# Layer 1 of a two-layer decoder trunk on one core: one order list from keys to turn, scalings shared by three engines, adaLN gate summed through DRAM

## The chip, the cores and the metric

The kernel runs on one core of a Trainium2 chip. The metric is device time in microseconds (us) of one execution. TensorE (PE) has a row of its own for weight loads (PEld); the others are VectorE (DVE), ScalarE (ACT), GpSimd (POOL), and SyncE (SP), which here only issues DMAs. Every engine takes its instructions in order.

## The reference

The trunk has 256 tokens of width 1024 and two layers. Both do x = x + gate * mixer(rmsnorm(x) * (1 + scale) + shift), where shift, scale and gate come from c @ ada_w + ada_b. Layer 1 is sparse attention with 16 heads in 4 groups; layer 2 is a chunkwise mLSTM with 8 heads. A final RMSNorm follows. What matters here, cut from the reference:

```python
shift, scale, gate = jnp.split(c @ ada_w[i] + ada_b[i], 3, axis=-1)
h = rmsnorm(x, norm_g[i]) * (1.0 + scale[:, None, :]) + shift[:, None, :]
q, kv, gate_logits, z = jnp.split(h @ w_in, A_SPLITS, axis=-1)
k_cmp = compress_tokens(kv[:, :, 0], ...); v_cmp = compress_tokens(kv[:, :, 1], ...)
p_cmp = masked_probs(s_cmp, dist_c >= 0)        # compressed branch
p = masked_probs(s, mask)                       # selected branch, then the window branch
o = gates[:, :, 0] * o_cmp + gates[:, :, 1] * o_slc + gates[:, :, 2] * o_win
y = o.reshape(B, S, A_WIDTH) * jax.nn.silu(z)
x = x + gate[:, None, :] * (y @ w_out)
```

masked_probs is a softmax: exponentials of the scores less a row's extreme, divided by their sum. The products keep more than one float32r pass's precision: each factor is split into hi (rounded to fp32r) and lo (the rest), and a product is the three matmuls hi*hi, lo*hi, hi*lo.

## The kernel before, in words

Layer 1 is written with a manual schedule: an engine runs its instructions in the order in which the program text makes them. It has four stages. `first_phase` loads x and c and makes the modulated, transposed activations (to about 52 us). The key stage in `nsa` (to 71 us) multiplies them with eight blocks of key and value weights (`kv_block`, L539 to L541; the loop runs over all eight, and behind each it makes embeddings or splits queries). `attention` (to about 157 us) runs over eight pairs of heads n = 0 to 7, driven by the string ORDER: each word of it is one step, and the number behind it names the pair, the head j in it, and the branch. `turn` (to about 186 us) ends layer 1: output projection, residual, RMSNorm, transposition and the first products of layer 2. Layer 2 is ordered by a scheduler and runs to 421 us.

The steps of `attention`, with the lines of the profile: S, scores (PE, L754 and L757); m, a row's extreme (DVE, L773); e, exponential with its sum (ACT, L780); f, factors gate/sum (DVE, L786 to L788); the **scalings** s, p, q, which multiply 128x128 and 128x256 probabilities by a factor for each row (L794; s on DVE, p on POOL, q one branch on each); T, transposes of the scaled probabilities (PE, L799) and t, their copy out of PSUM (ACT, L624); V, probabilities times values, in matmuls packed by columns (PE, L816); C, the compressed branch (PE, L821); y, times the SiLU of z (DVE, L825); Y, hi and lo of y (L624, L829); z, the gate path (PE, L1610 to L1612), whose weights are split in two halves of 512 columns each by `make_hi` on ACT (L164) and `make_lo` on DVE (L169); out and last, the output projection (PE, L869); `hi` and `lo` alone split the next weights in the stream; d, a column of the shift and scale sums for layer 2 (DVE, L852).

The **gate of layer 1**: `gr` multiplies c by four weight blocks in column-packed matmuls (PE, L226, two halves of 512 columns), which leaves four partial rows on four partitions; `gc` copies them to SBUF (ACT); `gs` sums them and spreads the sum to all 128 partitions by a matmul with a 0/1 matrix `sel` in fp32 (PE, L859); `ga` adds it to the bias that an ACT-queue DMA has spread into `gate0` (DVE, L863; step `bias`, L855). `gate0` is first read by the residual's multiplication (DVE, L1067).

`turn` is ordinary code: for each half a of the tokens the residual (L1067, L1068), squares (ACT, L1111), the root (ACT L209, DVE L210 to L214), the normalisation (ACT L1115, DVE L1116), eight transposes (PE, L1125), the modulation (ACT L1137, DVE L1135), rounding to hi (DVE L1145, ACT L1143), the rest lo (DVE, L1149), and layer 2's first products (PE, L1158).

Weights come by DMAs on SP's queue, 512 KB each, in the order of a list `queue`, into a ring of buffers; POOL's queue carries small loads and layer 2's exchanges through DRAM scratch.

## Time and profile before

| what | value |
| --- | --- |
| time, median of 3 runs | 423.61 us (423.51 to 425.01) |
| profiled execution, its own time | 423.31 us |
| its span in the trace | 421.5 us |
| granted TensorE clock | 0.996 |
| PE, PEld busy | 98%, 85% |
| DVE, ACT, POOL busy | 83%, 64%, 23% |

The span is what the trace covers; 1.8 us of the execution's time lie outside it. A busy share is over the whole span. The chain of waits follows the work that ended last back to what released it. The groups of instructions give the count, the busy time and the mean duration of a form. The windows give busy times stage by stage. The DMA issues give the median time from issue to landing. On PE durations overlap, since matmuls are pipelined; the distance from one start to the next says what an instruction costs there.

### The profile page before, as it was taken

The numbers are of one execution on the slowest core, as the hardware profiler recorded it, in microseconds if no ns is written. First come the engines' busy times: TensorE is split into PE (matmuls) and PEld (weight loads), VectorE is DVE, ScalarE is ACT, GpSimd is POOL, SyncE is SP. The second block draws the span as 40 slices with busy tenths as digits, with TensorE's granted clock in tenths as the row PEclk, the third lists the DMA queues.
The fourth block names the chain that finished last, engine by engine and source line by source line (L and its number), as shares of the span: only waits on it lengthen the run. The fifth ranks groups of instructions, "written<-read, shape, count | busy, mean of one in ns | idle before, by whom it ended". The sixth has DMA issues, their size and how long they took to land.

```text
span 421.5 us, 7600 instructions
## 1 busy us (share of the span) xinstructions
PE 412.3 (98%) x2669; PEld 357.2 (85%) x2669; DVE 348.6 (83%) x736; ACT 270.8 (64%) x541; POOL 96.6 (23%) x154
## 2 busy tenths in 40 slices
PE   8999999999999999999999999999999999999994
PEld 5899999789778877878999999888888888888884
DVE  6999898999999998878592699899858998558554
ACT  6666693788987973668547966565456554565523
POOL 4000112354676750142223200000000240320000
PEclk9999999999999999999999999999999999999998
DMA  8999996963799678239667467467456587640002
GB/s 321 410 407 406 396 322 197 342 274 136 253 334 388 236 251 298 96 119 317 218 226 277 157 193 225 177 205 265 169 176 202 186 296 230 180 143 0 0 2 100
DMA packets 27543, 96.21 MB, mean 228 GB/s; under 512 B 3512, under 2 KB 3616, under 8 KB 27376
## 3 DMA queue, kind: packets, MB, share of 16 engines
q1 hardware_dynamic: 26208, 92.30, 61.9%
q0 software_dynamic: 1008, 2.63, 1.7%
q10 hardware_dynamic: 288, 0.79, 0.5%
q8 instruction: 21, 0.34, 0.3%
q14 instruction: 18, 0.15, 0.1%
HBM read 94.61 MB, written 1.09 MB: 227 GB/s over the span
## 4 chain that ended last, share of the span: by engine, by line
PE 84%; issue 5%; DMA 4%; POOL 2%; DVE 2%; ACT 1%; SPq 0%; DVEq 0%; POOLq 0%
PE bank L539 10%; PE bank L541 10%; PE bank L540 10%; PE bank L433 7%; PE bank L1612 6%; PE bank L1610 6%; PE bank L1611 6%; PE bank L1523 5%; PE bank L1036 5%; PE bank L1158 3%; DMA Q<-in_columns 3%; PE bank L799 2%; PE bank L1403 2%; PE bank L816 2%; PE bank L754 2%
## 5 line engine op out<-in xcount | busy, mean ns | idle before, releaser
L169 DVE TENSOR_TENSOR wl<-raw,wh 128x1024 fp32r<-128x1024 f32 (+4 forms) x127 | 139.3, 1112 | 34.5 <-ACT wh L164 33.8
L164 ACT ACTIVATE wh<-raw 128x1024 fp32r<-128x1024 f32 (+4 forms) x127 | 119.2, 957 | 65.1 <-PE bank L541 28.2
L539 PE MATMUL bank<-wh,one 128*128 128x512 f32 (+1 forms) x208 | 76.9, 370 | 0.0
L540 PE MATMUL bank<-wl,one 128*128 128x512 f32 (+1 forms) x208 | 76.3, 367 | 0.0
L541 PE MATMUL bank<-wh,one 128*128 128x512 f32 (+1 forms) x208 | 76.2, 367 | 0.0
L1610 PE MATMUL bank<-one,wh 128*128 128x256 f32 x208 | 59.6, 287 | 0.0
L1612 PE MATMUL bank<-one,wl 128*128 128x256 f32 x208 | 59.0, 284 | 0.1
L1611 PE MATMUL bank<-one,wh 128*128 128x256 f32 x208 | 58.8, 283 | 0.0
L794 POOL TENSOR_SCALAR Pr<-Pr,f 128x128 f32<-128x128 f32 (+1 forms) x42 | 46.7, 1128 | 32.9 <-DVE f L788 18.8
L539 PEld LDWEIGHTS bank<-wh,one 128*128 128x128 f32 x208 | 39.2, 188 | 6.2 <-DVE tz L511 0.2
L541 PEld LDWEIGHTS bank<-wh,one 128*128 128x128 f32 x208 | 39.2, 188 | 6.2
L540 PEld LDWEIGHTS bank<-wl,one 128*128 128x128 f32 x208 | 39.2, 189 | 6.0
L1610 PEld LDWEIGHTS bank<-one,wh 128*128 128x128 f32 x208 | 39.7, 191 | 1.4 <-issue 0.8
L1612 PEld LDWEIGHTS bank<-one,wl 128*128 128x128 f32 x208 | 39.7, 191 | 0.5 <-DVE wl L169 0.3
L1611 PEld LDWEIGHTS bank<-one,wh 128*128 128x128 f32 x208 | 39.8, 191 | 0.1
L780 ACT ACTIVATE Pr<-Pr,mn 128x128 f32<-128x128 f32 (+1 forms) x64 | 28.2, 444 | 4.3 <-DVE mn L773 4.3
L433 PE MATMUL bank<-one,wh 128*128 128x256 f32 x224 | 29.8, 284 | 0.5 <-ACT one L407 0.4
L433 PEld LDWEIGHTS bank<-one,wh 128*128 128x128 f32 x224 | 28.1, 192 | 0.9 <-ACT one L407 0.6
L160 POOL TENSOR_TENSOR raw<-raw,gate 128x256 f32<-128x256 f32 x16 | 13.6, 858 | 49.7 <-DMA raw<-in_out_b 24.9
L1384 DVE SCALAR_TENSOR_TENSOR conv<-bank,one,conv 128x255 f32<-128x255 f32 (+2 forms) x48 | 20.0, 466 | 2.1 <-ACT conv L1379 2.1
L852 DVE CUSTOM_DVE_ANT_0 raw<-raw,one,one 128x1024 f32<-128x1024 f32 x16 | 21.1, 1330 | 0.0
L773 DVE CUSTOM_DVE_ANT_0 Pr<-bank,one 128x128 f32<-128x128 f32 (+1 forms) x64 | 18.7, 348 | 0.0
(336 smaller groups left out, 793.1 us busy)
## 6 DMA issues: line engine op xcount, KB each, us to landing
raw<-in_wide SPq DMA_DIRECT2D x44, 512.0 KB, 4.4
raw<-in_units SPq DMA_DIRECT2D x18, 512.0 KB, 4.6
raw<-in_turn SPq DMA_DIRECT2D x16, 512.0 KB, 6.8
raw<-in_gates SPq DMA_DIRECT2D x16, 512.0 KB, 4.9
raw<-in_out_b SPq DMA_DIRECT2D x16, 512.0 KB, 3.9
raw<-in_start SPq DMA_DIRECT2D x8, 512.0 KB, 9.7
Q<-in_columns SPq DMA_DIRECT2D x8, 512.0 KB, 9.6
raw<-in_hidden SPq DMA_DIRECT2D x8, 512.0 KB, 4.3
```

What stands on the lines that cost most here:

```text
L164: self.nc.scalar.activation(v(hi), src, AF.Copy)
L169: self.nc.vector.tensor_sub(v(lo), src, v(hi).bitcast(F32))
L433: nc.tensor.matmul(out, w[:, ch * P : ch * P + P], h[:, kk], start=(kk == 0 and m == 0 and ch % 2 == 0), stop=(kk == 7 and m == 2), skip_g ...
L539: nc.tensor.matmul(out, self.hh[:, kk, sl], wh, start=first, stop=False, skip_group_check=True)
L540: nc.tensor.matmul(out, self.hh[:, kk, sl], wl, start=False, stop=False, skip_group_check=True)
L541: nc.tensor.matmul(out, self.hl[:, kk, sl], wh, start=False, stop=last, skip_group_check=True)
L780: nc.scalar.activation(v, v, AF.Exp, bias=mn[:, a, br, j : j + 1], scale=-1.0, accum_out=sm[:, a, br, j : j + 1])
L794: es[br].tensor_scalar(v, v, F[n][:, a, br, j : j + 1], None, op0=OP.mult)
L852: nc.vector.tensor_tensor_reduce(raw, raw, self.cbc, scale, self.pca[:, 72 + 8 * b + kc : 73 + 8 * b + kc], OP.mult, OP.add, self.cols1[s] ...
L1610: nc.tensor.matmul(out, wh, self.hh[:, kk], start=first, stop=False, skip_group_check=skip)
L1611: nc.tensor.matmul(out, wh, self.hl[:, kk], start=False, stop=False, skip_group_check=skip)
L1612: nc.tensor.matmul(out, wl, self.hh[:, kk], start=False, stop=last, skip_group_check=skip)
```

## The change

One list for layer 1 from the first key block to the turn: `kv_block` is cut in three parts for each block (`k:block,part`), queries (`qa`, `qb`), embeddings (`E`), and the evacuations (`kd`, `G`, `vo`) become words of ORDER; so do the turn's steps (`l` last, `r` and `rp` residual on DVE or POOL, `sq` square, `sc` root, `x` normalise, `tr` transpose, `md` modulate, `ro` rounded, `re` rest, `n` and `v` products, `nh` and `nl` splits). The whole of ORDER is new. Six of the eight key blocks are now loaded as part of the stream's `hi` words. The scalings are named by the engines of the two branches (`spv`: POOL and DVE; `saa`: ACT twice): POOL goes from 42 to 32 instructions, DVE from 22 to 14, and ACT has 18 as a copy with a factor from a column. The gate's two `sel` matmuls, its two additions and the spread of the bias by an ACT-queue DMA go; instead five DMAs on POOL's queue do the sum through DRAM: `g1` twice (a store of four rows), `g2` (a load as 32 x 4 x 32), a DVE sum and addition of the bias on 32 partitions (`g3`), `g4` (a store of 32x32), `g5` (a load of the whole row into all 128 partitions of `gate0`, 512 KB). The weights of z are laid out so that hi and lo are one instruction each of 1024 columns in place of two of 512. Line numbers move by about 15 to 20 (L794 becomes L816, L799 L821, L816 L838, L1067 L1093, L1135 L1151).

```diff
@@ make_hi
-        if kind == "z":
-            r4 = raw.rearrange("p k j (i d) -> p k j i d", i=2)
-            views = [((lambda w, i=i: w.rearrange("p (k i j d) -> p k i j d", k=4, i=2, j=2)[:, :, i]), r4[:, :, :, i]) for i in range(2)]
-        elif kind == "q":
+        if kind == "q":
...
@@ nsa
-        def kv_block(kk):
-
-            wh, wl = self.take()
+        kw, banks = [], {}
+
+        def kv_block(kk, part):
+
+            while len(kw) <= kk:
+                kw.append(self.take())
...
     ORDER = """
-    d:0,0 hidden:0 hi hidden:1 S:0,0 lo S:0,1 hi hidden:2 hidden:3 z:0,0 m:0,0 m:0,1 e:0,0 lo S:1,0 e:0,1 f:0 gelu:0 s:0,0 hi S:1,1 gelu:1
...
+    k:0,1 hi hi lo lo hi lo qa:3 k:0,0 k:0,2 k:1,0 d:0,0 qa:2 k:1,1 k:1,2 E:1,0 hi k:2,1 k:3,1 qb:3 hi k:2,2 k:2,0 k:3,0 k:4,0 lo lo E:0,0 hi lo E:1,1
...
+    l:0,0,6 l:0,0,7 r:0,0 sq:0,0 l:0,1,6 l:0,1,7 r:0,1 sq:0,1 l:1,0,3 l:1,1,3 l:1,0,4 nl:2 sc:0 l:1,0,5 x:0,1 nh:1 l:1,0,6 l:1,0,7 nl:1 l:1,1,4 rp:1,0
...
@@ attention
         def scaled(n, j, *es):
             for br in range(2):
                 for a in range(2):
-                    v = probs(n, j, br, a)
-                    es[br].tensor_scalar(v, v, F[n][:, a, br, j : j + 1], None, op0=OP.mult)
+                    v, f = probs(n, j, br, a), F[n][:, a, br, j : j + 1]
+                    if es[br] is nc.scalar:
+                        copy(v, v, scale=f)
+                    else:
+                        es[br].tensor_scalar(v, v, f, None, op0=OP.mult)
...
-        def gate_bias():
-            nc.scalar.dma_start(self.gate0, t["ada_b"][0:1, 2048:3072].partition_broadcast(P))
-
-        def gate_sum(bank):
-            b = B["gs"] = self.bank(bank)
-            nc.tensor.matmul(b, self.sel, W["A"].pop(0), start=True, stop=True)
-
-        def gate_add(n):
-            g = self.gate0[:, 512 * n : 512 * n + 512]
-            nc.vector.tensor_tensor(g, g, B["gs"], op=OP.add)
+        def four(A):
+            return A.rearrange("(j r) k -> j r k", r=32)[:, 0]
+
+        def gate_store(n):
+            if not n:
+                W["quarters"] = self.pd.tile([4, D], F32, name=self.nm("quarters"), tag="quarters")
+            nc.gpsimd.dma_start(W["quarters"][:, 512 * n : 512 * n + 512], four(W["A"].pop(("gate", n))))
+
+        def gate_load():
+            W["gq"] = T([32, 4, 32])
+            nc.gpsimd.dma_start(W["gq"], W["quarters"].rearrange("j (b c) -> b j c", b=32))
+
+        def gate_sum():
+            W["gv"] = T([32, 32])
+            nc.vector.tensor_reduce(W["gv"], W["gq"].rearrange("b j c -> b c j"), axis=AX.X, op=OP.add)
+            nc.vector.tensor_tensor(W["gv"], W["gv"], self.gbias, op=OP.add)
...
+            nc.gpsimd.dma_start(self.gate0, W["whole"].rearrange("b c -> (b c)").unsqueeze(0).partition_broadcast(P))
...
-               "s": lambda n, j: scaled(n, j, nc.vector, nc.vector), "p": lambda n, j: scaled(n, j, nc.gpsimd, nc.gpsimd), "q": lambda n, j: scaled(n, j, nc.vector, nc.gpsimd),
+               **{"s" + b + c: lambda n, j, b=b, c=c: scaled(n, j, by[b], by[c]) for b in "vpa" for c in "vpa"},
...
@@ turn
-        def last(a, half, ks):
-            for k in ks:
-                self.out_mm(k, *held[k], a, *pieces[a][half])
+        def last(a, half, k):
...
-        transposed(0)
-        for half in range(2):
-            last(1, half, [6, 7])
-        modulate(0)
-        hi(4)
-        rounded(0)
...
+        return {}, {"l": last, "sq": square, "sc": root, "x": scale, "tr": transposed, "md": modulate, "ro": rounded, "re": rest, "n": narrow, "v": wide,
...
-    out["path"] = flat([z[:, k, :, gp, :, ih] for ih in range(2) for gp in range(2) for k in range(2)])
+    out["path"] = flat([z[:, k, :, gp, :, ih].reshape(P, 4, 2, 2, 64).transpose(0, 1, 3, 2, 4) for ih in range(2) for gp in range(2) for k in range(2)])
```

Layer 2's order and `first_phase` up to its last instructions on PE are as they were. Three places where the rows moved:

PE at the first of the two gate sums, before. L226 are the packed rows of the gate, L757 and L754 the scores, L799 transposes, L859 the matmul with `sel` (`one_18` is that matrix, `adaA` the copied rows).

```order
L226 MATMUL bank_1605<-raw_1204,one_33_141 32x512
L757 MATMUL bank_1614<-KH_755,Q_946 128x256
L757 MATMUL bank_1614<-KL_756,Q_946 128x256
L757 MATMUL bank_1614<-KH_755,Q_946 128x256
L757 MATMUL bank_1614<-KL_756,Q_946 128x256
L799 MATMUL bank_1623<-one_16_89,Pr_1339 128x128 x3
L859 MATMUL bank_1637<-adaA_1629,one_18_94 128x512
L799 MATMUL bank_1642<-one_16_89,Pr_1504 128x128 x3
L754 MATMUL bank_1615<-KH_755,Q_946 128x512
L754 MATMUL bank_1615<-KL_756,Q_946 128x512
L754 MATMUL bank_1616<-KH_755,Q_946 128x512
L754 MATMUL bank_1616<-KL_756,Q_946 128x512
```

The same place in the change, behind the second half of the rows (now L223); L821 are transposes, L843 the compressed branch, L1578 the gate path.

```order
L223 MATMUL bank_1635<-raw_1518,one_33_140 32x512
L223 MATMUL bank_1635<-raw_1360,one_33_140 32x512
L223 MATMUL bank_1635<-raw_1460,one_33_140 32x512
L223 MATMUL bank_1635<-raw_1462,one_33_140 32x512
L223 MATMUL bank_1635<-raw_1518,one_33_140 32x512
L821 MATMUL bank_1662<-one_14_87,Pr_1508 128x128 x3
L821 MATMUL bank_1702<-one_14_87,Pr_1508 128x128 x3
L843 MATMUL bank_1532<-PcT_1582,one_264_1329 128x256
L843 MATMUL bank_1532<-PcT_1582,one_266_1330 128x256
L843 MATMUL bank_1532<-PcT_1582,one_264_1329 128x256
L843 MATMUL bank_1532<-PcT_1582,one_266_1330 128x256
L1578 MATMUL bank_1725<-one_4_70,wh_1162 128x256
```

No matmul with `sel` stands behind the rows any more, here or elsewhere: PE has 2136 rows in place of 2138.

POOL in the second half of `attention`, before: scalings of pairs 4 (`Pr_1631`, `Pr_1632`), one behind the other.

```order
L794 TENSOR_SCALAR Pr_1631<-Pr_1631,f_1752 128x128
L794 TENSOR_SCALAR Pr_1631<-Pr_1631,f_1752 128x256
L794 TENSOR_SCALAR Pr_1631<-Pr_1631,f_1752 128x128
L794 TENSOR_SCALAR Pr_1631<-Pr_1631,f_1752 128x256
L794 TENSOR_SCALAR Pr_1632<-Pr_1632,f_1752 128x128
L794 TENSOR_SCALAR Pr_1632<-Pr_1632,f_1752 128x256
L794 TENSOR_SCALAR Pr_1632<-Pr_1632,f_1752 128x128
L794 TENSOR_SCALAR Pr_1632<-Pr_1632,f_1752 128x256
```

POOL there in the change, from the store of the second half of the rows (L884) to the spread of the gate (L900); `Pr_1791` and `Pr_1792` are pair 5, `Pr_1946` pair 6, `Pr_2055` pair 7.

```order
L884 DMA quarters_1660<-adaA_1797 4x512
L888 DMA one_370_1827<-quarters_1660 32x4x32
L816 TENSOR_SCALAR Pr_1791<-Pr_1791,f_1872 128x128
L816 TENSOR_SCALAR Pr_1791<-Pr_1791,f_1872 128x256
L816 TENSOR_SCALAR Pr_1792<-Pr_1792,f_1872 128x128
L816 TENSOR_SCALAR Pr_1792<-Pr_1792,f_1872 128x256
L816 TENSOR_SCALAR Pr_1946<-Pr_1946,f_1979 128x128
L816 TENSOR_SCALAR Pr_1946<-Pr_1946,f_1979 128x256
L897 DMA whole_2150<-one_411_2006 32x32
L816 TENSOR_SCALAR Pr_2055<-Pr_2055,f_2146 128x128
L816 TENSOR_SCALAR Pr_2055<-Pr_2055,f_2146 128x256
L900 DMA gate_813<-whole_2150 128x1024
```

The load L888 reads what the two stores wrote, so it waits for the landing of the second, and the scalings of pairs 5 to 7 stand behind it on POOL.

DVE at the first half of the tokens in the turn, before, from the end of the root: L1116 normalises, `wl_2373` is the lo part of a 1024-column weight, L1135 modulates what PE transposed, L1145 rounds.

```order
L214 SCALAR_TENSOR_TENSOR rq_y_2362<-rq_a_2363,rq_y_2362 128x1
L1116 TENSOR_SCALAR Pr_2295<-one_2_69,rq_y_2362 128x512
L169 TENSOR_TENSOR wl_2373<-raw_2201,wh_2372 128x1024
L1135 TENSOR_SCALAR tz_2383<-bank_2382,cols_382_1915 128x128 x2
L1135 TENSOR_SCALAR tz_2383<-bank_2382,cols_424_2127 128x128 x2
L1145 CAST one_4_70<-tz_2377 128x4x128
L1067 TENSOR_TENSOR y_488_2413<-bank_2086,gate_813 128x512
L1149 TENSOR_TENSOR one_6_71<-tz_2377,one_4_70 128x4x128
L1067 TENSOR_TENSOR y_489_2418<-bank_2087,gate_813 128x512
L1068 TENSOR_TENSOR one_2_69<-one_2_69,y_489_2418 128x512
L1110 TENSOR_SCALAR ss_2224<-ss_2224,one_12_85 128x1
L1149 TENSOR_TENSOR one_6_71<-tz_2383,one_4_70 128x4x128
```

The same in the change (L1134 normalises, L1151 modulates, L1160 rounds, L1164 is the rest).

```order
L1134 TENSOR_SCALAR Pr_2326<-one_2_69,rq_y_2340 128x512
L166 TENSOR_TENSOR wl_2353<-raw_2170,wh_2352 128x816
L1093 TENSOR_TENSOR y_488_2371<-bank_2092,gate_813 128x512
L1151 TENSOR_SCALAR tz_2386<-bank_2385,cols_363_1789 128x128 x2
L1151 TENSOR_SCALAR tz_2386<-bank_2385,cols_433_2121 128x128 x2
L1160 CAST one_4_70<-tz_2376 128x4x128
L1164 TENSOR_TENSOR one_6_71<-tz_2376,one_4_70 128x4x128
L1093 TENSOR_TENSOR y_496_2427<-bank_2093,gate_813 128x512
L1094 TENSOR_TENSOR one_2_69<-one_2_69,y_496_2427 128x512
L1164 TENSOR_TENSOR one_6_71<-tz_2386,one_4_70 128x4x128
L1125 TENSOR_SCALAR ss_815<-ss_815,one_12_85 128x1
```

The 1024-column lo ahead of the modulation is gone; an 816-column one and the multiplication of the residual (L1093) stand there.

More of the change, by code (lines that the diff above doesn't have):

```diff
@@ L1107, in square, with narrow_hi, narrow_lo @@
+        def narrow_hi(n):
+            half_made[n] = self.make_hi(self.first + n)
+        def narrow_lo(n):
+            self.make_lo(*half_made.pop(n))
+            self._load()
+        def last(a, half, k):
+            while len(held) < k - 1:
+                n = len(held) + 2
+                held[n] = self.take(hold=n > 2)
+            self.out_mm(k, *held[k], a, *self.pieces[a][half])
         def square(a, half):
[L1108 removed]
@@ L1223, in turn, with narrow @@
-        rest(1, 0)
-        rest(1, 1)
-        lo(5)
-        w.append((4, self.take(hold=True)))
-        products(vs[0], w[2:], 0, 512, (0, 1))
-        products(bs[1][:, 0:272], first, 1, 272)
-        GT = self.T(pc, [P, 2, 16])
-        for a in range(2):
-            nc.vector.tensor_tensor(GT[:, a], bs[a][:, 256:272], self.bif, op=OP.add)
+        def narrow(a, m):
+            if not first:
+                first.extend((3 * n, self.take(hold=n > 0)) for n in range(3))
+            if not m:
+                bs[a] = self.bank(6 + a)
+            products(bs[a][:, 0:272], first, a, 272, (m,))
@@ L1233, in todo, with wide, gates @@
+        def wide(m, n):
+            if not vs:
+                vs.update((a, self.bank(4 + a)) for a in range(2))
+            while len(w) <= n:
+                w.append((2 * len(w), self.take(hold=True)))
+            products(vs[0], w[n : n + 1], 0, 512, (m,))
+        def gates(a):
+            if "t" not in half_made:
+                half_made["t"] = self.T(pc, [P, 2, 16])
+            nc.vector.tensor_tensor(half_made["t"][:, a], bs[a][:, 256:272], self.bif, op=OP.add)
         def todo():
```

311 lines of the change are left out of this document (129 added, 182 removed).

## The prediction

> **What bounds the kernel now.** First the page's busy times, then the chain of waits, because busy times alone do not say who waits for whom.
>
> ```profile
> PE 412.3 (98%) x2669; PEld 357.2 (85%) x2669; DVE 348.6 (83%) x736; ACT 270.8 (64%) x541; POOL 96.6 (23%) x154
> PE 84%; issue 5%; DMA 4%; POOL 2%; DVE 2%; ACT 1%; SPq 0%; DVEq 0%; POOLq 0%
> ```
>
> PE is 98% busy and carries 84% of the chain. The windows show whether another engine is as full where the change works:
>
> ```profile
> 90.00:110.00 20.00, 20.00 (x189) 15.99 (x188) 19.45 (x70) 16.83 (x54) 12.96 (x14) 1.00 0.36 129
> 110.00:130.00 20.00, 20.00 (x158) 15.99 (x157) 19.79 (x63) 15.71 (x51) 13.72 (x14) 1.00 0.94 344
> 130.00:150.00 20.00, 19.79 (x143) 16.30 (x143) 19.83 (x62) 17.52 (x49) 12.78 (x11) 1.00 0.79 293
> ```
>
> (Length, then PE, PEld, DVE, ACT, POOL; then clock, DMA share, GB/s.) DVE is as full as PE from 90 to 150 us, so who waits for whom decides. PE's waits from 52 to 187 us:
>
> ```profile
> PE bank L1158 <- DVE one L1145: 0.5, 1, 0.5
> PE bank L816 <- DVE y L825: 0.2, 1, 0.2
> PE bank L1158 <- DVE one L1149: 0.2, 1, 0.2
> ```
>
> PE waited 0.9 us in 135. DVE is full but keeps ahead. So layer 1 is as long as PE's list of matmuls, and only two things shorten it: fewer or cheaper matmuls, or these waits. The Trainium skill, Perfetto Trace Analysis, Identifying the Most-Contended Engine, says that matmul busy time is a bad measure because matmuls are pipelined, and that weight-load busy is the better one. By it PE would have 15% in hand (85%), and DVE would count as bound here; the 0.9 us of waits do not agree.
>
> **The change part by part.**
>
> *Gate sums off PE.* The order of the rows takes two fp32 matmuls with `sel` from PE and adds none.
>
> ```profile
> 109.82 0.67 PE bank L757 x4
> 110.49 0.33 PE bank L799 x3
> 110.82 0.98 PE bank L859 x2
> ...
> 113.39 0.47 PE bank L757 x4
> ...
> 129.66 0.86 PE bank L859 x2
> ```
>
> They held the chain for 0.98 + 0.86 = 1.84 us. Nothing lay beside them that PE waits for, so all of it goes: **-1.84**.
>
> *Fewer packed runs.* Four L757 matmuls take 0.67 us behind the packed L226, and 0.47 behind transposes: 0.20 for each return from a packed run. In the new order packed runs stand next to one another (a gate half beside V, V:6 beside V:7): by the rows of PE's order 9 runs in place of 11. **-0.4** (bounds 0 and 0.8, if entering a run costs as much as leaving it).
>
> *Waits that PE has.* One is at V:6 (L816 above), the others in the turn. Its timeline there:
>
> ```profile
> 170.93 0.85 PE L869 MATMUL bank<-KL,Q 128*128 128x512 f32 x3
> 171.61 0.84 PE L869 MATMUL bank<-KH,Q 128*128 128x512 f32 x3
> 172.52 1.24 PE L1158 MATMUL bank<-wh,one 128*128 128x272 f32 x8
> ...
> 179.71 1.09 PE L1158 MATMUL bank<-wh,one 128*128 128x512 f32 x4
> 181.29 0.97 PE L1158 MATMUL bank<-wh,one 128*128 128x272 f32 x5 [0.49 <-DVE one L1145]
> ```
>
> Three L869 go from start to start in 0.68 (170.93 to 171.61), 0.23 each. The run from 171.61 should have given way at 172.29 and did at 172.52: a fourth wait of 0.2 that has no bracket. The four matmuls from 179.71 take 0.93, so the last wait is 181.29 - 180.64 = 0.65, bracket and restart. In the turn that is 0.2 + 0.2 + 0.65 = 1.05, and 0.2 at V:6.
>
> Now each in the new order. V:6 waits for y:2's reading of its bank; in the new list five groups of three transposes (at 0.33) and nine projections (at 0.23) stand between `y:2` and V:6, 3.7 us: the 0.2 goes. In the turn, before the transposes 21 projections (4.9 us) stand behind the residual's last input where 18 did (4.2), so the root has 0.7 more. Between the first transposes and the products stand 9 matmuls (2.1 us) where 12 did (2.8), but what DVE has to do there is less:
>
> ```profile
> 169.53 1.23 DVE L169 TENSOR_TENSOR wl<-raw,wh 128x1024 fp32r<-128x1024 f32 x1 [1.15 <-ACT wh L164]
> 170.68 1.36 DVE L1135 TENSOR_SCALAR tz<-bank,cols 128x128 f32<-128x128 f32 x4
> 171.96 0.41 DVE L1145 CAST one<-tz 128x512 fp32r<-128x512 f32 x1
> ...
> 174.20 1.07 DVE L1068 TENSOR_TENSOR one<-one,y 128x512 f32<-128x512 f32 x1
> ...
> 175.64 0.68 DVE L1149 TENSOR_TENSOR one<-tz,one 128x512 fp32r<-128x512 f32 x1
> ```
>
> The modulation stood behind a lo of 1.23 us that itself waited 1.15 for ACT. Without it modulation and rounding are 1.36 + 0.41 and some 0.3 of handing over, 2.1 us against 2.1 of cover: about 0.1 left. In the second half 8 matmuls of 512 columns (1.9 us) cover what 6 (1.4) did: 0.65 falls to about 0.2. The L1149 wait: behind the rounding DVE now has a rest, a residual (a multiplication like L863 below and L1068) and the second rest, 0.68 + 0.68 + 1.07 + 0.68 = 3.1, and PE has 20 products of 272 columns (0.13 each: eight from 172.52 to 173.60) and two of 512 ahead of the need, 3.1: about 0.1 left. Together 1.05 becomes 0.4; with V:6 that is **-0.85** (bounds: -1.25, and 0 if as much comes back).
>
> *Scalings.*
>
> ```profile
> L794 POOL TENSOR_SCALAR Pr<-Pr,f 128x256 f32<-128x256 f32 x21 | 28.4, 1353 | 0.0
> L780 ACT ACTIVATE Pr<-Pr,mn 128x256 f32<-128x256 f32 x32 | 15.8, 498 | 3.2 <-DVE mn L773 3.2
> L794 POOL TENSOR_SCALAR Pr<-Pr,f 128x128 f32<-128x128 f32 x21 | 19.0, 904 | 32.9 <-DVE f L788 18.8 <-ACT PT L624 11.0 <-PE bank L799 3.2
> L780 ACT ACTIVATE Pr<-Pr,mn 128x128 f32<-128x128 f32 x32 | 12.4, 390 | 1.1 <-DVE mn L773 1.1
> L794 DVE TENSOR_SCALAR Pr<-Pr,f 128x256 f32<-128x256 f32 x11 | 4.4, 400 | 0.0
> L794 DVE TENSOR_SCALAR Pr<-Pr,f 128x128 f32<-128x128 f32 x11 | 3.9, 356 | 0.1
> ```
>
> POOL gives up five pairs (5 x 2.26 = 11.3 us), DVE four (3.0 us), ACT takes nine. ACT has no such form in this trace. Below: DVE's pair, 356 + 400 = 0.76; above: POOL's, 2.26 (20 us in all). I take the exponentials, same engine and shapes, also with a column as operand: 390 + 498 = 0.89 a pair, 8.0 us in all. ACT was busy 16.8 + 15.7 + 17.5 = 50.1 of 60 us from 90 to 150, and not every second of the 8 falls there. z gives some back:
>
> ```profile
> L164 ACT ACTIVATE wh<-raw 128x512 fp32r<-128x512 f32 x16 | 9.1, 628 | 0.0
> L164 ACT ACTIVATE wh<-raw 128x1024 fp32r<-128x1024 f32 x6 | 6.2, 1057 | 0.0
> L169 DVE TENSOR_TENSOR wl<-raw,wh 128x512 fp32r<-128x512 f32 x16 | 10.7, 708 | 0.0
> L169 DVE TENSOR_TENSOR wl<-raw,wh 128x1024 fp32r<-128x1024 f32 x6 | 7.4, 1247 | 0.0
> L863 DVE TENSOR_TENSOR gate<-gate,bank 128x512 f32<-128x512 f32 x2 | 1.4, 676 | 0.0
> ```
>
> 16 x 628 - 8 x 1057 = 1.6 us off ACT; 16 x 708 - 8 x 1247 = 1.4 off DVE. DVE also loses L863's 1.4 and gains a sum over 32x4x32 and an addition, of which I have no row: between 0.36 (one scaling of 128 columns) and 1.4 (as both L863), I take 0.7, as one L863. DVE is lighter by 3.0 + 1.4 + 1.4 - 0.7 = 5.1 us, ACT heavier by 6.4, POOL lighter by 11.3. None of the three holds the chain, so all this is worth **0** in itself: PE's matmuls hide it. If that cover is gone on ACT, 50.1 + 6.4 = 56.5 of 60 us still fits, but the copies t then queue behind scalings. For places with little lead in the new order (pair 3's transposes right behind its DVE scaling, out:0 into banks that m:7,1 has to free) I add **+0.3** (bounds 0 and 3).
>
> *The gate through DRAM.* The prices of such hops:
>
> ```profile
> raw<-in_start SPq DMA_DIRECT2D x8, 512.0 KB, 9.7
> DT<-in_final_g POOLq DMA_DIRECT2D x1, 512.0 KB, 4.8
> drawer<-one POOLq DMA_DIRECT2D x1, 16.0 KB, 3.6
> ```
>
> What POOL spends on an issue, and what PE does meanwhile:
>
> ```profile
> L1343 POOL DMA_DIRECT2D QK<-drawer x4 | 2.2, 559 | 3.2 <-DMA drawer<-one 3.2
> ```
>
> ```profile
> 124.00 2.75 PE bank L816 x32
> ...
> 128.07 0.94 PE bank L754 x4
> ```
>
> g2 waits on POOL for the landing of g1's second store, 3.6 us by `drawer`, and the scalings of pairs 5 to 7 queue behind it; T:5,0,0 waits for the first of them (2.26). From the transposes that gate the copy of the rows to T:5,0,0 PE has two heads' scores (0.94 + 0.47 each), four words of z and C:1 (at 0.12 a 128x256 matmul 12 and 4 of them: 1.44 each, 0.48), 32 packed (2.75) and four L799 (1.3): some 13 us. The wait asks for t and the copy (no more than the 0.63 of a 512-column split each), 3.6, an issue of 0.56 and 2.26: 7.7. So 5 us are left. Then g4 (3.6) lies beside 5.8 us (twelve projections, five groups of transposes, 16 packed of V:5), and g5 (4.8) beside 7.7 (32 packed of V:6 and V:7, C:3, transposes, 18 projections) until L1067 wants the gate; behind g5 on POOL only one residual queues. **0**, with bounds of 0 and the lateness priced below. The Trainium skill speaks against the change here: DMA: Bandwidth & Descriptors, Anatomy of one DMA, says that a DMA's semaphore wait is done on the issuing sequencer before dispatch, and gives 2.0 us + bytes/436e3 a hop, most of it a receipt from memory. That would make 2.0 of the 3.6; the `drawer` row is dearer, and the row decides.
>
> *Key stage, layer 2.* The same key matmuls in another order; the waits of PE quoted at the start hold none from it: **0**. Layer 2's rows are the same.
>
> **Sum:** -1.84 - 0.4 - 0.85 + 0.3 = -2.8. The span goes from 421.5 to 418.7; with the 1.8 us outside it 420.5, against 423.3 for this profiled execution. The median of the runs stood 0.3 above it; runs scatter by about as much, so I add 0.1: **420.6**, against 423.4 on the same footing.
>
> **The rivals.** (1) *Only the matmuls go*: every wait removed comes back elsewhere, since the same chains between DVE, ACT and PE are only put in another order. For it: DVE is at 19.8 of 20. Against it: DVE is lighter by 5. 423.4 - 1.84 = 421.6. (2) *ACT becomes late*: a scaling ahead of a copy t on ACT delays the transposed probabilities; six of the nine pairs late by half a pair's scaling, 0.45, take back 2.7: 423.3. For it: 56.5 of 60 us. Against it: ACT's scalings take 0.9 where POOL's took 2.3. (3) *DVE was the bound after all*, as the skill's weight-load rule would have it: the time falls with DVE's 5.1 us, 423.4 - 5.1 = 418.3; the waits speak against it. (4) *Slower: the gate arrives late*. Place: g4 and g5 on POOL's queue and then L1067. From when: both with their issues longer than 5.8 + 7.7 and the root's 0.7, 14.2 us. By the rows they take 3.6 + 4.8 + 1.1 = 9.5. Were both as slow as 512 KB at the start (9.7, DMA engines full), they would take 20.5, be 6.3 late, and give 426.9. For it: DMA shares of 0.79 to 0.94 from 110 to 150. Against: the POOL queue's row of the same size has 4.8. (5) The change does not do what it says: excluded for PE, whose order shows the matmuls gone.
>
> **How the numbers follow.** Forecast 0.60 (419.3 to 421.6), rival 1 0.14, rival 2 0.11, rival 3 0.06, rival 4 0.09. About 0.5% (2.1 us) is what a measurement of this kernel tells from no change: faster is below 421.5, slower above 425.7. Faster: nearly all of the forecast (0.56), half of rival 1 (0.07), rival 3: 0.69. Same: the rest of both (0.11) and rival 2: 0.22. Slower: rival 4, 0.09. The range runs from rival 3 to just past rival 2, 418.3 to 423.7, and leaves out rival 4 and the ends of the others; the forecast alone is 419.3 to 421.6.
>
> **What would show it.** Right: no matmul of 128x512 between transposes behind the packed gate rows; PE's waits from 52 to 187 us at 0.5 or less in sum; the scaling on ACT near 390 and 498 ns; POOL idle some 3 us at g2 with PE not waiting for T:5,0,0; no DVE wait for `gate` before its first residual. Wrong: PE waits for PT (ACT's copies) or for `one` in the turn of 0.5 and more, or DVE idle at L1093 for a DMA. If the time is above 421.6, the step that failed is the +0.3 for tight places or the -0.85.

## The result, and the profile after

The changed kernel takes 421.38 us (median of 6 runs, 420.66 to 422.19), against 423.61 for the kernel before on the same chip (6 runs, 423.50 to 425.01): a ratio of 0.994, 95% interval 0.9922 to 0.9957. The forecast was 420.6 with a range of 418.3 to 423.7. The profiled execution took 421.66 us, its span is 419.9, and the granted clock is 0.996 as before.

The page of the changed kernel, busy times and shares of the chain of waits:

```profile
PE 409.9 (98%) x2665; PEld 355.9 (85%) x2665; DVE 344.7 (82%) x720; ACT 276.0 (66%) x551; POOL 92.3 (22%) x149
PE 90%; DMA 4%; ACT 2%; DVE 1%; issue 1%; SPq 1%; DVEq 0%; ACTq 0%
```

PE is 2.4 us less busy, and its share of the chain rose from 84% to 90%. The total lies in the forecast; where it comes from is not what was forecast. PE's timeline shows it at three places: the first matmul of the key stage, layer 2's first matmul behind the turn, and the last matmul of the kernel. Before:

```profile
52.38 0.28 PE L1610 MATMUL bank<-one,wh 128*128 128x256 f32 x1
...
192.27 0.39 PE L540 MATMUL bank<-wl,one 128*128 128x512 f32 x1
...
415.76 0.28 PE L1523 MATMUL bank<-late,V 128*128 128x256 f32 x1
```

After:

```profile
52.22 0.36 PE L540 MATMUL bank<-wh,one 128*128 128x256 f32 x1
...
188.71 0.39 PE L541 MATMUL bank<-wl,one 128*128 128x512 f32 x1
...
414.09 0.28 PE L1491 MATMUL bank<-late,V 128*128 128x256 f32 x1
```

From the key stage to the end of the turn (called layer 1 below) PE took 192.27 - 52.38 = 139.89 us, and now takes 136.49: **-3.4**, where -2.8 was forecast. From there to the last matmul it took 223.49 and now takes 225.38: **+1.9**, where nothing was forecast, since layer 2's rows are the same. So two questions stand: why layer 2 became slower, and of what the -3.4 is made.

**Layer 1.** PE's waits between 50 and 192 us, by the view of waits:

```profile
PE bank L1173 <- ACT wh L161: 0.5, 1, 0.5
PE bank L821 <- ACT PT L643: 0.3, 1, 0.3
```

The view leaves out short idle times; from start to start they show. Measured so, the four waits that were to be shortened cost 0.22 + 0.36 + 0.65 in the turn and 0.37 at V:6, 1.6 us. Three are gone, and the one of 0.65 (PE at 176.75, behind the rounding) is down to 0.19: 1.4 us went. Two others came. The first is at 118 us, where the transposes of pair 3 need a bank that ACT has to copy out first. The chain of waits there (start, length, what):

```profile
105.33 1.85 PE bank L223 x16
107.18 0.43 PE bank L821 x3
107.62 6.34 DMA raw<-in_path
...
113.98 1.06 ACT wh L161
115.04 1.97 ACT Pr L799 x8
117.01 0.95 ACT wh L161
117.96 0.38 ACT PT L643
...
118.47 0.52 PE bank L821 x3
```

Read from below: the transposes waited for the copy (L643), the copy stood on ACT behind a split of weights (L161), that behind exponentials and a first split, and the first split behind its weights, which landed at 113.96. SP's queue had waited for a buffer that the packed gate rows (L223) read until 107.2. One late load thus holds up a `hi` that the order puts ahead of a copy, and a copy that PE needs stands behind it. The second wait is in the turn:

```profile
177.17 4.49 PE bank L1173 x27
...
181.69 1.07 ACT wh L161
...
182.80 4.91 PE bank L1173 x20
```

The split at 181.69 writes a buffer that the narrow products (272 columns) read until then, and PE needs its result at once. From start to start these two waits cost 0.46 and 0.69; at the same place before stood 0.23.

### The profile page after: what moved, and what is told of

Read it like the earlier page. It is cut to its first block, busy times and chain, and to the rows that moved or that the text cites. A ratio compares the mean times of both kernels' runs of the same rounds, so it can differ in the third digit from the quotient of the medians.

```text
span 419.9 us, 7581 instructions
## 1 busy us (share of the span) xinstructions
PE 409.9 (98%) x2665; PEld 355.9 (85%) x2665; DVE 344.7 (82%) x720; ACT 276.0 (66%) x551; POOL 92.3 (22%) x149
## 4 chain that ended last, share of the span: by engine, by line
PE 90%; DMA 4%; ACT 2%; DVE 1%; issue 1%; SPq 1%; DVEq 0%; ACTq 0%
PE bank L540 10%; PE bank L542 10%; PE bank L541 10%; PE bank L430 8%; PE bank L1580 6%; PE bank L1578 6%; PE bank L1579 5%; PE bank L906 5%; PE bank L1491 5%; PE bank L1062 5%; PE bank L1173 4%; PE bank L838 3%; PE bank L821 2%; DMA Q<-in_columns 2%; PE bank L1371 2%; PE bank L575 2%
## 5 line engine op out<-in xcount | busy, mean ns | idle before, releaser
L161 ACT ACTIVATE wh<-raw 128x1024 fp32r<-128x1024 f32 (+3 forms) x119 | 118.4, 1008 | 72.2 <-PE bank L542 35.6
L540 PE MATMUL bank<-wh,one 128*128 128x512 f32 (+2 forms) x208 | 77.8, 374 | 0.0
L541 PE MATMUL bank<-wl,one 128*128 128x512 f32 (+2 forms) x208 | 77.0, 370 | 0.0
L542 PE MATMUL bank<-wh,one 128*128 128x512 f32 (+2 forms) x208 | 76.8, 370 | 0.0
L1578 PE MATMUL bank<-one,wh 128*128 128x256 f32 x208 | 59.3, 285 | 0.0
L816 POOL TENSOR_SCALAR Pr<-Pr,f 128x128 f32<-128x128 f32 (+1 forms) x32 | 37.6, 1195 | 32.4 <-DVE f L807 22.4
L1578 PEld LDWEIGHTS bank<-one,wh 128*128 128x128 f32 x208 | 39.2, 188 | 0.4 <-DVE xT L965 0.2
L1579 PEld LDWEIGHTS bank<-one,wh 128*128 128x128 f32 x208 | 39.3, 189 | 0.2
L799 ACT ACTIVATE Pr<-Pr,mn 128x128 f32<-128x128 f32 (+1 forms) x64 | 28.2, 451 | 1.6 <-DVE mn L792 1.6
L430 PEld LDWEIGHTS bank<-one,wh 128*128 128x128 f32 x224 | 27.7, 188 | 1.1 <-ACT one L404 0.6
```

The lines of the kernel that those rows point to most:

```text
L161: self.nc.scalar.activation(v(hi), src, AF.Copy)
L430: nc.tensor.matmul(out, w[:, ch * P : ch * P + P], h[:, kk], start=(kk == 0 and m == 0 and ch % 2 == 0), stop=(kk == 7 and m == 2), skip_g ...
L540: nc.tensor.matmul(out, self.hh[:, kk, sl], wh, start=first, stop=False, skip_group_check=True)
L541: nc.tensor.matmul(out, self.hh[:, kk, sl], wl, start=False, stop=False, skip_group_check=True)
L542: nc.tensor.matmul(out, self.hl[:, kk, sl], wh, start=False, stop=last, skip_group_check=True)
L799: nc.scalar.activation(v, v, AF.Exp, bias=mn[:, a, br, j : j + 1], scale=-1.0, accum_out=sm[:, a, br, j : j + 1])
```

## Experiments

Stage lengths are compared rather than ends where a profile is read, since the start of the key stage, in a part of the kernel that no edit touches, lies anywhere from 52.1 to 53.6 us in these profiles. "Layer 1" and "layer 2" are the two distances above. Each ratio is to runs of the kernel before on the same chip, whose medians were 423.43 to 423.82 us.

### Why layer 2 slowed: the place of the weights

One thing in the change reaches what layer 2 multiplies: the bias of the gate is now a tile `gbias` of 32 x 32 fp32 in the pool of constants `pc`. That pool lies ahead of the weights' ring of buffers, so `raw`, `wh` and `wl` begin 128 bytes higher in every partition (82176 for the first `wh`, where it was 82048). The activations that layer 2 multiplies them with stayed where they were (from 12672 and 20864).

**gbias_elsewhere**: the same tile, in a pool that lies behind.

```diff
-        self.gbias = self.T(pc, [32, 32])
+        self.gbias = self.T(self.p1, [32, 32])
```

> The changed kernel with one edit: the 128 bytes per partition of the gate's bias are taken from another region of SBUF, behind the weight buffers and no longer ahead of them, so that the weight buffers (raw, wh, wl) lie where they lay before the change. Instructions and their order are those of the changed kernel. Theory A (place of the weights): layer 2 runs 1.9 us longer after the change because a matmul of a 128x512 weight on the activations goes from 227.8 to 232.5 ns start to start once wh and wl lie 128 bytes further on; here it is back near 228, layer 2 is 1.9 us shorter, and the time is about 419.5. Theory B (the pace differs from execution to execution or from chip to chip, whatever the kernel): the time stays at 421.4 and the pace follows no pattern.

420.36 us (419.63 to 420.63, 4 runs), ratio to before 0.992 [0.9908, 0.9933]; span 417.9. The interval overlaps the changed kernel's, but layer 2 is 223.47, as before the change.

**before_padded**: the opposite, the kernel before with an unused tile of the same size in `pc`.

```diff
+        self.pad = self.T(pc, [32, 32])
+        g.memset(self.pad, 0.0)
```

> The kernel before with one edit: 128 bytes per partition that nothing reads are taken ahead of the weight buffers, so that these lie where they lie after the change (GpSimd sets the bytes once at the start). Theory A (place of the weights): the 128x512 matmuls of layer 2 go from about 228 to 232.5 ns, layer 2 takes 1.9 us more, time about 425.5. Theory B (pace by execution or chip): 423.6, unchanged.

424.88 us (424.73 to 425.48, 5 runs), ratio 1.0033 [1.0021, 1.0045]. Layer 2 is 225.41. Its rows are those of the kernel before; what differs is the place of the weights and of the other tiles behind the pad, and one memset on POOL at the start.

**shift_256**: the changed kernel with the tile twice as large, so that the weights begin 256 bytes higher than before.

```diff
-        self.gbias = self.T(pc, [32, 32])
+        self.gbias = self.T(pc, [32, 64])[:, 0:32]
```

> The changed kernel with 128 more unused bytes per partition ahead of the weight buffers, which thus lie 256 bytes behind their place before the change. Theory (relative place of weights and activations by 256 bytes): the 128x512 matmuls of layer 2 are back near 228 ns and the time near 420.4, as with the bias elsewhere. Rival 1 (period of 512 bytes or more): they stay at 232 or take another value, time 421.4. Rival 2 (any shift costs): 232, 421.4.

419.64 us (419.35 to 420.85, 5 runs), ratio 0.9901 [0.9887, 0.9915]; layer 2 is 223.46. In the medians the three edits are worth -1.0, +1.3 and -1.7 us, less than the 1.9 of the profiles; the intervals of the last two are clear of the kernels that they are compared with.

The groups of instructions by form, from 190 to 420 us, one of the three lines of 512-column matmuls of each kernel (count, busy time, mean ns). Before, after, `gbias_elsewhere`, `before_padded`, `shift_256`, one fence each:

```profile
L541 PE MATMUL bank<-wh,one 128*128 128x512 f32 x160 | 62.2, 390 | 0.0
```

```profile
L541 PE MATMUL bank<-wl,one 128*128 128x512 f32 x158 | 62.3, 395 | 0.0
```

```profile
L541 PE MATMUL bank<-wl,one 128*128 128x512 f32 x158 | 61.7, 390 | 0.0
```

```profile
L542 PE MATMUL bank<-wl,one 128*128 128x512 f32 x160 | 63.1, 395 | 0.0
```

```profile
L541 PE MATMUL bank<-wl,one 128*128 128x512 f32 x160 | 62.4, 390 | 0.0
```

Each 512-column matmul takes 5 ns more where the weights lie 128 bytes higher, and as long as before where they lie 256 higher. From start to start it is 227.8 ns and 232.5; over 480 matmuls the 4.7 ns are 2.3 us, and the 384 of 256 columns give 0.3 back (281 for 283 on one of their three lines). So layer 2's +1.9 is shown to be the place of the weights; 0 and 256 bytes cost the same, and 128 do not. The rival that the pace goes by chip or by execution is out: kernels of both places ran on each of two chips, and their profiles part by place. Nothing in the order of the rows could have told it.

### The terms of the sum

**gate_by_matmul**: the changed kernel with the two `sel` matmuls, their additions and the spread of the bias put back in place of the DMAs.

```diff
-    ... cdist:1 cexp ... g1:0 ... g1:1 ... g2 ... g3 ... g4 ... g5 ...
+    ... cdist:1 bias cexp ... gs:0 ga:0 ... gs:1 ga:1 ...
```

> The changed kernel with the gate of layer 1 summed as before: two fp32 matmuls with the 0/1 matrix, two additions on VectorE, the bias spread by a DMA on ScalarE's queue; the five DMAs through DRAM on GpSimd's queue are out. Everything else as changed, the weights' place too. My step says that the matmuls held PE for 1.84 us and nothing else waits for the gate: 421.4 + 1.8 to 2.2 = 423.2 to 423.6. The rival (the gain came from the order, the matmuls fell into waits that are there anyway) says 421.4. If GpSimd's waits at the DRAM hops cost something after the change, the time rises by less than 1.84.

423.03 us (422.8 to 424.2, 12 runs), ratio 0.9987 [0.9979, 0.9996]. That is 1.65 more than the changed kernel, for -1.84 forecast. In the profile layer 1 is 137.78, 1.29 longer, but the wait for pair 3's copy is 0.31 there (too short for the view) in place of 0.46: 1.4 on the same footing.

**only_gate_changed**: the kernel before, in its old order, with the gate through DRAM alone (and the bias in the pool behind, so that the weights stay in their place).

```diff
-    ... bias cexp ... gs:0 ga:0 ... gs:1 ... ga:1 ...
+    ... cexp ... g1:0 ... g1:1 ... g2 ... g3 g4 ... g5 ...
```

> The kernel before with one part of the change alone: the gate of layer 1 goes through DRAM (five DMAs on GpSimd's queue, the sum on VectorE) in place of the two matmuls, the two additions and the ScalarE-queue DMA; the order of everything else and the place of the weights are those of before. In the list of before, g1 stands where the first sum stood and behind the second copy, g2 behind the scalings of pair 5, g5 behind the last scalings. My step (-1.84 us of PE work, nothing waits for the hops): 423.7 - 1.8 = 421.9. Rival (in the old order the scalings of pairs 6 and 7 on GpSimd have no lead for the hold at g2, about 2 us of the 5.6 us hop): transposes of pair 6 wait, 422.5 to 424.

424.41 us (423.8 to 425.39, 11 runs), ratio 1.0015 [1.0006, 1.0023]: no gain at all from taking the matmuls off PE in this way, above both expectations and 3.0 above the changed kernel. PE's waits from 50 to 192 us:

```profile
PE bank L817 <- DVE y L826: 0.9, 1, 0.9
PE bank L800 <- POOL Pr L795: 0.9, 2, 0.5
PE bank L800 <- ACT PT L625: 0.7, 1, 0.7
```

Where 0.9 us were waited in all before, these three alone are 2.5. Part of that is my placement of the first store. POOL's timeline of this kernel, and of the kernel before, at pair 3's scalings:

```profile
110.80 0.62 POOL L861 DMA_DIRECT2D quarters<-adaA  x1 [4.11 <-PE bank L800]
111.47 3.99 POOL L795 TENSOR_SCALAR Pr<-Pr,f 128x128 f32<-128x128 f32 x4
```

```profile
107.52 4.92 POOL L794 TENSOR_SCALAR Pr<-Pr,f 128x128 f32<-128x128 f32 x4 [0.72 <-DVE f L788]
```

The store waits on POOL for its rows, and the four scalings behind it start at 111.5 rather than 107.5; PE lost 1.27 us there, start to start. The wait for DVE's `y` at V:6, 0.72 more than before, is placement too: DVE's sum of the gate stood for the load.

```profile
138.73 0.39 DVE L869 TENSOR_REDUCE one<-one 32x32 f32<-32x128 f32 x1 [0.84 <-DMA one<-quarters]
```

With that `y` starts 1.16 us later than in the kernel before (150.06 for 148.90), where PE is 0.43 later. The third wait, 0.86 for ACT's copy at 130 us, is the old order's own: the second `sel` matmul held PE for 0.86 us while ACT finished that copy (129.43 to 130.30 in the kernel before), so without the matmul PE waits for the copy. With a last 0.2 all new waits are 3.05; less 1.84 that is 1.2, and layer 1 is 141.07 for 139.89. So this run shows for one of the two sums that it cost nothing in the old order. What the old order would have gained with the new steps in better places was not run.

**scalings_off_scalar**: the changed kernel with ACT's nine pairs of scalings back on POOL.

```diff
-    ... sap:0,1 spa:1,0 ... sap:2,0 ... spa:4,0 sap:4,1 ... saa:6,0 spa:6,1 ... sav:7,0 ...
+    ... spp:0,1 spp:1,0 ... spp:2,0 ... spp:4,0 spp:4,1 ... spp:6,0 spp:6,1 ... spv:7,0 ...
```

> The changed kernel with the nine pairs of scalings that it gives to ScalarE put back on GpSimd, at the same places of the list. My step says that the scalings are worth 0 in themselves, since PE's matmuls hide them: 421.4. Rival: in this order GpSimd (2.3 us a pair) cannot serve them in time; where both branches of a head or both heads of a pair fall on it (pairs 1, 4, 6, 7), transposes wait 2 to 4 us each: 427 to 433. If so the split over three engines is what lets the new order stand, and 0 was the price of the wrong question.

430.69 us (430.01 to 431.23, 4 runs), ratio 1.0155 [1.0139, 1.0172]: 9.3 us above the changed kernel. Its waits, and the windows (length, PE, PEld, DVE, ACT, POOL; then clock, DMA share, GB/s):

```profile
PE bank L821 <- POOL Pr L816: 4.7, 5, 1.7
PE bank L821 <- ACT PT L643: 0.9, 1, 0.9
```

```profile
90.00:110.00 20.00, 17.70 (x171) 13.82 (x170) 17.32 (x59) 14.70 (x49) 10.15 (x12) 1.00 0.34 116
110.00:130.00 20.00, 19.09 (x161) 15.56 (x158) 16.89 (x58) 15.64 (x50) 15.25 (x14) 1.00 0.93 357
130.00:150.00 20.00, 17.37 (x114) 14.46 (x113) 15.97 (x56) 13.48 (x41) 16.49 (x16) 0.91 0.51 172
```

POOL is nowhere full (16.5 of 20 us at most), and yet PE waits for it five times: the new order leaves no room for a scaling of 2.3 us a pair where one of 0.9 was planned. Layer 1 is 144.90, 8.4 us longer. From start to start the waits in attention make 7.3 us, where the changed kernel has 0.46. The rest is the granted clock, right behind two of them that make 2.2 us:

```profile
140.00:145.00 5.00, 5.00 (x30) 3.65 (x30) 2.13 (x6) 1.75 (x3) 5.00 (x5) 0.70 0.85 282
```

From 139.5 to 143.0 us a 128x256 matmul takes 214 to 222 ns from start to start, and 118 to 120 before and behind: half the pace for 3.5 us, an estimated 1.7 us. In the new order, then, ACT's scalings are not worth 0 but a condition of the rest.

### The two new waits

**split_behind_copy**: two `hi` words of the list, each moved behind the copy or the scalings that PE waits for.

```diff
-    ... m:4,1 hi e:4,1 hi d:1,2 T:3,0,1 t:3,0,1 C:0 f:4 spa:4,0 sap:4,1 d:1,3 ...
+    ... m:4,1 e:4,1 hi d:1,2 T:3,0,1 t:3,0,1 C:0 f:4 spa:4,0 sap:4,1 hi d:1,3 ...
```

> The changed kernel with two words of the list moved: of the two splits of gate-path weights that stand among the exponentials of pair 4 and the copies of pair 3, the first goes behind the exponential of head 1, the second behind the scalings of pair 4. Theory: PE's one new wait in attention (0.46 us at 117.9, a transposed copy of pair 3 late on ScalarE) comes from ScalarE, which stood 0.68 us at the first split for a weight load and then ran both splits ahead of that copy; here it goes: 421.4 - 0.45 = 421.0, and PE waits for no copy there. Rival: the wait is ScalarE's load as a whole (the nine pairs of scalings); then it only moves on to a later copy, and the time stays at 421.4.

420.69 us (420.57 to 421.91, 5 runs), ratio 0.9937 [0.9926, 0.9949], whose interval overlaps the changed kernel's. Layer 1 is 135.68, 0.8 shorter, and the view has only the other wait:

```profile
PE bank L1173 <- ACT wh L161: 0.5, 1, 0.5
```

The chain of waits speaks for the split ahead of the copy, but this run does not show it: with the old places of `hi` the wait is 0.46 in the changed kernel, 0.62 in `shift_256`, 0.31 in `gate_by_matmul` and absent in `gbias_elsewhere`, one profile each. It is there in some executions; that it hangs on when the loads land is argued from the chain.

**three_mends**: this, the tile `gbias` elsewhere, and the narrow products of the second half in the order hh*wh, hl*wh, hh*wl, with the rest ahead of the lo, so that `wh` comes free earlier.

```diff
-    ... v:2,1 ro:1,0 nl:5 v:0,2 re:1,0 params re:1,1 v:1,2 n:1,0 ...
+    ... v:2,1 ro:1,0 re:1,0 params re:1,1 nl:5 v:0,2 v:1,2 n:1,0 ...
-   l, v = ((self.hh, wh), (self.hl, wh), (self.hh, wl))[m if n == 512 else (0, 2, 1)[m]]
+   l, v = ((self.hh, wh), (self.hl, wh), (self.hh, wl))[m if n == 512 or a else (0, 2, 1)[m]]
```

> The changed kernel with three edits: the gate's bias lies behind the weight buffers; the two splits of gate-path weights stand behind the exponential and the scalings; and in the turn the second half's narrow products run hi*hi, lo*hi, hi*lo in place of hi*hi, hi*lo, lo*hi (with the rests ahead of the last split on VectorE), so that the hi buffers of the narrow weights come free 1.0 us earlier. Theory: the three costs are separate. Place of the weights -1.0 by the runs (1.9 by the trace), splits -0.7, and PE's wait of 0.69 us for a split weight at 182 us, behind a buffer that the narrow products hold, falls to about 0.1: 421.4 - 1.0 - 0.7 - 0.6 = 419.1. Rival: the wait for the buffer only moves (VectorE's rests become late for lo*hi, 0.5 us): 419.7.

419.40 us (418.6 to 419.83, 4 runs), ratio 0.9887 [0.9873, 0.9901]. The view has no wait of PE left between 50 and 192 us; layer 1 is 135.10, layer 2 is 223.47. The time lies between the two that were expected. Against the changed kernel that is -1.4 and -1.9 by the profiles and -2.0 in the medians; its profiled execution began the key stage 1.4 us later.

### How far the place of operands goes

Layer 1's output projection multiplies `Q` with `wh` and `wl`. Its pace, 233 ns from start to start, is that of the slow place, before and after the change alike.

**three_mends_q**: `three_mends` with 96 bytes more behind `gbias`, which moves `Q` to the same remainder modulo 256 as the weights.

```diff
+        self.gbias = self.T(self.p1, [32, 56])[:, 0:32]
```

> The kernel of the three mends with 96 bytes per partition added ahead of the attention's buffers, so that the buffers Q (the other factor of the output projection) come to the same remainder by 256 bytes as the weights wh and wl. Theory (relative place by 256 bytes): the 128x512 matmuls of the output projection go from 232 to about 228 ns as those of layer 2 did, some 110 of them: 0.5 us less than the kernel of the three mends. Rival (only the absolute place of the weights counts): no difference, 232 ns stays.

418.62 us (418.28 to 419.61, 4 runs), ratio 0.9875 [0.986, 0.989]. The projection's pace falls to 228.6 ns; layer 1 is 134.69. The intervals of the two ratios overlap, so the gain in time is not shown; the pace is.

**shift_64**, **mends_and_64**, **mends_and_192**: the weights 64 or 192 bytes higher than before, the first on `gbias_elsewhere`, the others on `three_mends_q`. The pad has 16 columns for 64 bytes, and 48 for 192.

```diff
+        self.pad = self.T(pc, [P, 16])
+        g.memset(self.pad, 0.0)
```

> The changed kernel with the bias elsewhere and 64 unused bytes per partition ahead of the weight buffers, which then lie 64 bytes off the remainder by 256 that they share with the activations (0 off gave 228 ns for a 128x512 matmul of layer 2, 128 off gave 232.5). Theory 1 (any offset that is not a multiple of 256 costs the same): 232.5 ns, 421.4 less the noise. Theory 2 (the cost grows with the offset): about 230 ns, 420.8. Theory 3 (a period of 64): 228 ns, 420.4 or a little under.

417.78 us (416.97 to 418.6, 4 runs), ratio 0.9855 [0.9835, 0.9876]. None of the expectations holds as it stands: the 512-column matmuls take 228 to 234 ns by line, and the 256-column ones fall from 120.0 to 114.6. Layer 2 is 221.99, 1.5 shorter than at the old place.

> The kernel of the three mends with Q at the weights' remainder by 256 bytes (418.6), and the 64 unused bytes ahead of the weight buffers. Theory (place and order are separate costs): offset 64 brings 256-column matmuls on the activations from 120 to 114.6 ns and takes 512-column ones from 228.8 to 230.8, as it did without the mends (420.4 to 417.8, -2.6): 418.6 - 2.6 = 416.0. Rival: the faster PE runs into ScalarE's and VectorE's lateness in attention (0.41 and 0.63 us of waits showed without the mends): 416.5 to 417.5.

417.45 us (416.95 to 417.74, 4 runs), ratio 0.9854 [0.9839, 0.9868]. This is the fastest kernel of the study, but not clear of `shift_64` or `three_mends_q`, whose intervals its own overlaps. Neither expectation has its mechanism: the 256-column matmuls of layer 2 go at 117.5 ns, not at 114.6, and layer 2 is 223.42. The gain is in layer 1, 133.71.

> The same with 192 unused bytes in place of 64. Theory 1 (only the distance to a multiple of 128 counts): as with 64, 114.6 ns for 256 columns and about 416. Theory 2 (each offset has its own pace): other values; a 256-column matmul at 118 to 120 and the time at 418 to 420.

419.33 us (419.09 to 419.59, 4 runs), ratio 0.9898 [0.9881, 0.9914]; layer 2 is 225.17, close to that with 128. That is the second expectation, other values for each offset: 118 ns for 256 columns.

The 256-column group of `shift_64` and of `mends_and_64`, and the 512-column one of `mends_and_192`:

```profile
L1580 PE MATMUL bank<-one,wh 128*128 128x256 f32 x128 | 35.5, 277 | 0.0
```

```profile
L1580 PE MATMUL bank<-one,wh 128*128 128x256 f32 x128 | 36.0, 281 | 0.0
```

```profile
L543 PE MATMUL bank<-wl,one 128*128 128x512 f32 x156 | 61.7, 396 | 0.0
```

All fourteen profiles, by how much higher than in the kernel before the weights begin:

| weights higher by, bytes | kernels | layer 2, us |
| --- | --- | --- |
| 0 or 256 | before, gbias_elsewhere, only_gate_changed, three_mends, three_mends_q, shift_256 | 223.46 to 223.50 |
| 128 | after, before_padded, gate_by_matmul, split_behind_copy, scalings_off_scalar | 225.26 to 225.41 |
| 192 | mends_and_192 | 225.17 |
| 64 | shift_64; mends_and_64 | 221.99; 223.42 |

The two orders of layer 1 and both ways of summing the gate stand in the first two rows, and layer 2 does not ask which it was. Why the two kernels at 64 differ by 1.4 us stays open: weights and activations of layer 2 begin at the same bytes in both, so the place of these operands is not all.

Two other groups of matmuls in these profiles settle what the pace goes by. The projection takes 228.5, 227.9 and 228.0 ns in `three_mends_q`, `mends_and_64` and `mends_and_192`, where `Q` and the weights share a remainder modulo 256 that is itself 128, 192 and 64; in the other kernels it takes 233 to 234, except 229.6 in `only_gate_changed`, where `Q` begins 64 bytes below the weights, as layer 2's activations do in the two kernels with 64 bytes. (The places are those of the built kernels.) And layer 2's 512-column matmuls of `wh` with `V`, two buffers that move together, take 228 to 229 ns in all fourteen profiles. So it is the distance of the two operands that counts here, and not the place of either alone.

## Why the prediction was right in the time and wrong in a step

The time, the sign and the likeliest case came true, by two errors of opposite sign: 0.6 us too little for layer 1, and 1.9 for layer 2 left out. That the sum still fell into the range of the likeliest case is in part luck.

- **The step that failed: layer 2, 0.** "Layer 2's rows are the same" is true of the rows and was taken for the time. It is +1.9 us, by 128 bytes of place. The prediction named the tight places and the waits as what to suspect first if the time came out high; neither would have led there. `gbias_elsewhere`, `before_padded` and `shift_256` did.
- **Gate sums off PE, -1.84**: 1.65 in the medians, 1.4 by the profiles. But "nothing lay beside them that PE waits for, so all of it goes" is wrong for the old order: beside the second sum lay a copy on ACT, and its 0.86 us came back as a wait.
- **Waits, -0.85**: mis-sized. Of 1.6 us 1.4 went. The estimate left 0.4 over where 0.19 stayed (the 0.2 for the second half was right), and it started from 1.25: it read the wait for L1149 and the one at V:6 as 0.2 each by their brackets, where start to start says 0.36 and 0.37.
- **Tight places, +0.3**: 0.46 at pair 3's transposes, one of the two places named, though behind ACT's copy and a late load rather than DVE's scaling; and 0.46 more (0.69 for 0.23) at a place in the turn that was not named. Together 0.9, within the bounds of 0 and 3. That PE would wait 0.5 or less in sum is wrong by the view of waits, 0.8.
- **Fewer packed runs, -0.4**: right. From start to start, a full-array matmul next to a packed run takes up to 0.1 us more than others of its form, waits apart (a 128x256 behind one 222 ns for 120); 18 such places where there were 22 make -0.4, and the packed runs themselves are 0.15 shorter. With -1.84 - 1.4 + 0.9 that is -2.9 of the -3.4, and 0.5 stays without a cause.
- **Scalings, 0**: none of the three engines holds the chain, as said. But the term asked what moving them costs, and not what the new order would be without it: 9.3 us, 1.7 of them by a lower clock. Their durations were right to 2% on ACT:

```profile
L816 POOL TENSOR_SCALAR Pr<-Pr,f 128x256 f32<-128x256 f32 x16 | 20.5, 1284 | 0.0
L643 ACT ACTIVATE Pr<-Pr,f 128x256 f32<-128x256 f32 x9 | 4.5, 503 | 0.0
L643 ACT ACTIVATE Pr<-Pr,f 128x128 f32<-128x128 f32 x9 | 3.6, 397 | 0.1
L816 DVE TENSOR_SCALAR Pr<-Pr,f 128x256 f32<-128x256 f32 x7 | 2.6, 371 | 0.0
L816 DVE TENSOR_SCALAR Pr<-Pr,f 128x128 f32<-128x128 f32 x7 | 2.0, 283 | 0.0
```

The exponentials' 498 and 390 stood for ACT's 503 and 397.

- **The gate through DRAM, 0**: right; PE waits for none of its hops. Their prices, from the DMA issues (KB, median us to landing):

```profile
gate<-whole POOLq DMA_DIRECT2D x1, 512.0 KB, 5.5
...
quarters<-adaA POOLq DMA_DIRECT2D x2, 8.0 KB, 5.4
store<-QK POOLq DMA_DIRECT2D x2, 8.0 KB, 1.8
...
one<-quarters POOLq DMA_DIRECT2D x1, 16.0 KB, 3.4
whole<-one POOLq DMA_DIRECT2D x1, 4.0 KB, 4.2
```

The prediction put g1's store and g4 at 3.6 each and g5 at 4.8, and had no price for g2's landing; they took 5.4, 4.2, 5.5 and 3.4. POOL's timeline shows the wait at the load, not 3 us as forecast:

```profile
122.95 0.58 POOL L884 DMA_DIRECT2D quarters<-adaA  x1
129.16 0.59 POOL L888 DMA_DIRECT2D one<-quarters  x1 [5.63 <-DVE mn L792]
```

(The bracket names a DVE instruction; the store's landing at 128.55 is what it waited for.) The scalings of pair 5 stand behind these 5.6 us, and the 5 us of room that were worked out there took 2 of them. The gate had landed at 154.63, and its first reader started at 160.4, 5.8 us later. The Trainium skill, DMA: Bandwidth & Descriptors, Anatomy of one DMA, says that a DMA's wait on a semaphore is done by the issuing sequencer; the trace agrees, since POOL stood for it. By its 2.0 us + bytes/436e3 a hop, an estimate for the gate's stores is 2.0, where 4.2 and 5.4 were measured; two stores of 8 KB in layer 2 (`store<-QK`) took 1.8.

- **Rival 1** (what goes from PE comes back as waits) is true in the old order for the second sum, 0.86 of 1.84. **Rival 2** (a copy behind scalings on ACT) did not show: the one late copy, 0.46 and not 2.7, stood behind splits of weights and a late load. **Rival 3**: the Trainium skill, Perfetto Trace Analysis, Identifying the Most-Contended Engine, reads PE's load by weight-load busy time. Before the change that is 80 to 82% in attention (16.0 to 16.3 of 20 us), where DVE has 97 to 99%, so DVE would be the bound there; the 85% in the prediction is over the whole span, where DVE has 83. The waits do not agree (0.9 us in 135 before, 0.8 in 140 after). **Rival 4**: the gate was not late. ACT and DVE after the change, over the stage where ACT was put at 56.5 of 60 us:

```profile
sum 60.00, PE 59.70 PEld 48.91 DVE 57.08 ACT 53.92 POOL 32.31; mean PE 19.90 PEld 16.30 DVE 19.03 ACT 17.97 POOL 10.77
```

ACT is at 53.9 (50.1 before) and DVE at 57.1 (19.45 + 19.79 + 19.83 = 59.1 before): both have 3 to 6 us of 60 free. Over the whole span DVE became lighter by 3.9 us (5.1 were forecast), ACT heavier by 5.2 (6.4) and POOL lighter by 4.3 (11.3).
